# RMSNorm over 16384 rows: squares on ScalarE alone, a third of the rows scaled by GpSimd, and an instruction order written out by hand

## The chip, the cores and the metric

The kernel runs on one core of a Trainium2 chip. The metric is the device time of one execution in microseconds; the median of several executions is given. A core has a VectorE (DVE), a ScalarE (ACT), a GpSimd (POOL), a TensorE (PE) and sixteen DMA engines; SP is the engine that issues most of the transfers here. Each engine works through its own instructions in order, and engines wait for one another by semaphores. SBUF and PSUM are the on-chip memories, both of 128 partitions.

## The reference

```python
x = randn(16, 1024, 512) in float32; gamma = ones(512)

def reference(x, gamma):
    eps = 1e-5
    rms = sqrt(mean(x ** 2, axis=-1, keepdims=True) + eps)
    return x / rms * gamma
```

Each of 16384 rows of 512 numbers is divided by the root of its mean square and multiplied by gamma. The input is read once, 33.5 MB, and the output written once, 33.5 MB.

## The kernel before

The rows are cut into four blocks t = 0 to 3. In a block each of the 128 partitions holds R = 32 neighbouring rows, 64 KB. SBUF has three slots of one block (line 39); blocks 0, 1 and 2 go into slots 0, 1 and 2, and block 3 goes into slot 0 again when block 0 has been stored. The scaling is done in place, so a slot is loaded, scaled and stored.

Work goes in groups of G = 8 rows, 16 groups in all. `row_stats` (line 63) makes the inverse root mean square of a group. It has two ways, in turn. Even groups square row by row on ScalarE, which adds up each row itself (`accum_out`, line 76). Odd groups square four rows at a time into a PSUM tile `sq` (line 70), and VectorE sums each row (line 71). Then ScalarE takes the square root (line 82) and VectorE the reciprocal (line 83). `apply` (line 86) scales the eight rows on VectorE, one `scalar_tensor_tensor` a row (line 88): slot times `rstd`, a number for each partition, times `gamma_b`, gamma spread over all partitions in SBUF. A matmul by a column of ones (line 55) and a copy (line 57) make `gamma_b` at the start.

The last loop computes the statistics of the following group ahead of the scaling of the present one. The framework's scheduler then sets the order on each engine; in the trace, reductions, rows and reciprocals of neighbouring groups are mixed.

`transfers` (line 100) issues all loads and stores on SP's queue, in this order: loads of block 0 (rows 0 to 7, then 8 to 31) at the start; after group (0,0) the store of row 0, the load of block 1, half the load of block 2, the store of row 1, the other half; after block 0's last group its remaining rows in two stores and the load of block 3 in two halves, each of which waits until the store from the same place in slot 0 has landed; after block 1's last group its store (8.4 MB); after block 2's last group its store (8.4 MB); and block 3 in two stores. SP issues in this order, and an issue that must wait holds those behind it.

Of the kernel before, what the change touches and what calls it, by code (L numbers as in the profile page):

```python
# [1 line left out]

# [4 lines left out]


@with_exitstack
def kernel(  # L10
    ctx: ExitStack,
    tc: tile.TileContext,
    x: bass.AP,
    gamma: bass.AP,
    out: bass.AP,
):
    nc = tc.nc
    P = nc.NUM_PARTITIONS
    eps = 1e-5
    fp32 = mybir.dt.float32  # L20
    AF = mybir.ActivationFunctionType
    OP = mybir.AluOpType

    xf = x.flatten_outer_dims()
    of = out.flatten_outer_dims()
    N, D = xf.shape
    R = 32
    G = 8
    H = 4
    assert N == 4 * P * R  # L30

    xv = xf.rearrange("(t p r) d -> t p r d", p=P, r=R)
    ov = of.rearrange("(t p r) d -> t p r d", p=P, r=R)

    const = ctx.enter_context(tc.tile_pool(name="const", bufs=1))
    stats = ctx.enter_context(tc.tile_pool(name="stats", bufs=4))
    psum = ctx.enter_context(tc.tile_pool(name="psum", bufs=2, space=bass.MemoryType.PSUM))

    slots = [const.tile([P, R, D], fp32, name=f"slot{i}") for i in range(3)]

    def load(t, slot, r0, r1):
        nc.sync.dma_start(out=slots[slot][:, r0:r1], in_=xv[t][:, r0:r1])  # L42

    def store(t, slot, r0, r1):
        nc.sync.dma_start(out=ov[t][:, r0:r1], in_=slots[slot][:, r0:r1])

    load(0, 0, 0, 8)
    load(0, 0, 8, 32)

    gamma_row = const.tile([1, D], fp32)  # L50
    nc.scalar.dma_start(out=gamma_row, in_=gamma.unsqueeze(0))
    ones_col = const.tile([1, P], fp32)
    nc.vector.memset(ones_col, 1.0)  # L53
    gamma_psum = psum.tile([P, H, D], fp32, name="sq")
    nc.tensor.matmul(gamma_psum[:, 0], ones_col, gamma_row, start=True, stop=True)  # L55
    gamma_b = const.tile([P, D], fp32)
    nc.vector.tensor_copy(out=gamma_b, in_=gamma_psum[:, 0])  # L57

    eps_t = const.tile([P, 1], fp32)
    nc.vector.memset(eps_t, eps)  # L60
    sq_scratch = const.tile([P, D], fp32)

    def row_stats(slot, g):
        ss = stats.tile([P, G], fp32, name="ss")
        rms = stats.tile([P, G], fp32, name="rms")
        rstd = stats.tile([P, G], fp32, name="rstd")
        if (g // G) % 2:
            for h in range(0, G, H):
                sq = psum.tile([P, H, D], fp32, name="sq")
                nc.scalar.activation(out=sq, in_=slots[slot][:, g + h : g + h + H, :], func=AF.Square)  # L70
                nc.vector.tensor_reduce(  # L71
                    out=ss[:, h : h + H], in_=sq, axis=mybir.AxisListType.X, op=OP.add
                )
        else:
            for r in range(G):
                nc.scalar.activation(  # L76
                    out=sq_scratch,
                    in_=slots[slot][:, g + r, :],
                    func=AF.Square,
                    accum_out=ss[:, r : r + 1],  # L80
                )
        nc.scalar.activation(out=rms, in_=ss, func=AF.Sqrt, bias=eps_t, scale=1.0 / D)  # L82
        nc.vector.reciprocal(out=rstd, in_=rms)  # L83
        return rstd

    def apply(slot, g, rstd):
        for r in range(G):
            nc.vector.scalar_tensor_tensor(  # L88
                out=slots[slot][:, g + r, :],
                in0=slots[slot][:, g + r, :],  # L90
                scalar=rstd[:, r : r + 1],
                in1=gamma_b,
                op0=OP.mult,
                op1=OP.mult,
            )

    groups = [(t, g) for t in range(4) for g in range(0, R, G)]
    slot_of = [0, 1, 2, 0]

    def transfers(t, g):  # L100
        if (t, g) == (0, 0):
            store(0, 0, 0, 1)
            load(1, 1, 0, 32)
            load(2, 2, 0, 16)
            store(0, 0, 1, 2)
            load(2, 2, 16, 32)
        elif (t, g) == (0, 24):
            store(0, 0, 2, 16)
            store(0, 0, 16, 32)
            load(3, 0, 0, 16)  # L110
            load(3, 0, 16, 32)
        elif (t, g) == (1, 24):
            store(1, 1, 0, 32)
        elif (t, g) == (2, 24):
            store(2, 2, 0, 32)
        elif (t, g) == (3, 8):
            store(3, 0, 0, 16)
        elif (t, g) == (3, 24):
            store(3, 0, 16, 32)

    ahead = row_stats(0, 0)
    for k, (t, g) in enumerate(groups):
        rstd = ahead
        if k + 1 < len(groups):
            tn, gn = groups[k + 1]
            ahead = row_stats(slot_of[tn], gn)
        apply(slot_of[t], g, rstd)
        transfers(t, g)


# [1 line left out]
_INS = ['x', 'gamma']  # L132
_OUTS = [((16, 1024, 512), 'float32')]


# [23 lines left out]
```

## Time and profile before

| | |
|---|---|
| median of 3 runs | 162.24 us (162.03 to 162.33) |
| profiled execution, whole | 162.18 us |
| profiled execution, span from first to last instruction | 160.4 us |
| VectorE busy | 122.6 us, 163 instructions |
| ScalarE busy | 80.1 us, 162 instructions |
| GpSimd busy | 0.2 us, 4 instructions |
| TensorE busy | 2.0 us |
| moved by DMA | 67.13 MB, 418 GB/s over the span |
| HBM read and written | 33.56 and 33.55 MB |

The busy time of an engine says how much it worked, not whether the end waited for it. A line of a group gives source line, engine, operation, what it writes and reads with shapes, the count, then the total busy time in us, the mean of one in ns, and the idle time before it with what ended that. A line of the waits gives who waited for whom, the total in us, how often, and the longest. In the slices each digit is the busy share of a fortieth of the span, in tenths. A line of the timeline gives start, duration, engine, line and operation.

### The profile page before, as it was taken

How to read it: one execution, taken by the hardware profiler on the slowest of the kernel's cores; microseconds unless marked ns; L12 is line 12 of the kernel's file. 1: busy time of each engine (PE TensorE's matmuls, PEld its weight loads, DVE VectorE, ACT ScalarE, POOL GpSimd, SP SyncE). 2: the span in 40 equal slices, each digit the busy share in tenths (PEclk: the TensorE clock that was granted, in tenths of full speed). 3: DMA queues.
4: the chain of work that ended last, by engine and by line, in shares of the span. 5: the costliest groups of instructions: out<-in, count | busy, mean ns of one | idle time of the engine just before them, and what ended most of it. 6: DMA issues, size and time to landing. Idle time of an engine off the chain costs nothing.

```text
span 160.4 us, 410 instructions
## 1 busy us (share of the span) xinstructions
PE 2.0 (1%) x2; PEld 0.5 (0%) x2; DVE 122.6 (76%) x163; ACT 80.1 (50%) x162; POOL 0.2 (0%) x4
## 2 busy tenths in 40 slices
PE   4000000000000000000000000000000000000000
PEld 1000000000000000000000000000000000000000
DVE  0100928999999519999999999999999999994000
ACT  3098039990390999996900950079609940000000
POOL 0000000000000000000000000000000000000000
DMA  5999999699699999999999999998998998999993
GB/s 197 523 392 392 466 449 523 261 523 523 262 402 387 455 458 418 453 415 466 409 392 498 409 400 507 409 507 376 425 507 360 441 507 360 417 400 441 449 417 147
DMA packets 2164, 67.13 MB, mean 419 GB/s; under 512 B 241, under 2 KB 241, under 8 KB 498
## 3 DMA queue, kind: packets, MB, share of 16 engines
q1 hardware_dynamic: 2160, 67.11, 97.7%
q14 instruction: 2, 0.02, 0.0%
q10 hardware_dynamic: 2, 0.00, 0.0%
HBM read 33.56 MB, written 33.55 MB: 418 GB/s over the span
## 4 chain that ended last, share of the span: by engine, by line
DVE 67%; DMA 13%; ACT 7%; issue 2%; DVEq 0%; SPq 0%
DVE slot L88 48%; DVE ss L71 18%; DMA slot<-in_x_dram 13%; ACT sq_scratch L76 3%; ACT sq L70 3%; DVE rstd L83 1%; DVEq L154 0%; ACT rms L82 0%; SPq L42 0%
## 5 line engine op out<-in xcount | busy, mean ns | idle before, releaser
L88 DVE SCALAR_TENSOR_TENSOR slot<-slot,rstd,gamma_b 128x512 f32<-128x512 f32 x128 | 85.8, 738 | 0.1
L76 ACT ACTIVATE sq_scratch<-slot 128x512 f32<-128x512 f32 x64 | 40.0, 625 | 10.0 <-DMA slot<-in_x_dram 8.7
L70 ACT ACTIVATE sq<-slot 128x2048 f32<-128x2048 f32 x16 | 29.8, 1864 | 18.6 <-DVE ss L71 11.5
L71 DVE TENSOR_REDUCE ss<-sq 128x4 f32<-128x2048 f32 x16 | 35.9, 2274 | 3.4 <-ACT sq L70 3.4
L82 ACT ACTIVATE rms<-ss,eps_t 128x8 f32<-128x8 f32 x16 | 4.6, 297 | 25.9 <-DVE ss L71 25.7
L83 DVE RECIPROCAL rstd<-rms 128x8 f32<-128x8 f32 x16 | 3.1, 193 | 16.1 <-ACT rms L82 16.1
L76 ACT ACTIVATION_READ_ACCUMULATOR sq_scratch<-slot 128x1 f32 x64 | 11.9, 186 | 0.0
L57 DVE COPY gamma_b<-sq 128x512 f32<-128x512 f32 x1 | 0.7, 691 | 3.3 <-PE sq L55 3.3
L55 PE MATMUL sq<-gamma_row,ones_col 1*128 1x512 f32 x2 | 2.0, 1122 | 2.2 <-DMA gamma_row<-in_gamma_dram 2.2
L76 ACT ACT_TABLE_LOAD x1 | 1.3, 1283 | 1.3 <-PEq L143 1.3
L82 ACT ACT_TABLE_LOAD x1 | 1.3, 1283 | 0.0
L53 DVE MEMSET ones_col<- 1x128 f32 x1 | 0.2, 165 | 0.8 <-PEq L143 0.8
L55 PEld LDWEIGHTS sq<-gamma_row,ones_col 1*128 1x128 f32 x2 | 0.5, 306 | 2.2 <-issue 2.2
L143 POOL MEMSET const-bfloat16-1.0<- 128x1 bf16 x1 | 0.1, 101 | 0.0
L143 POOL MEMSET const-uint8-127<- 128x1 uint8 x1 | 0.1, 101 | 0.0
L143 POOL MEMSET const-float32-0.0<- 128x1 f32 x1 | 0.1, 98 | 0.2 <-issue 0.2
L143 POOL MEMSET const-float32-1.0<- 128x1 f32 x1 | 0.1, 98 | 0.0
L60 DVE MEMSET eps_t<- 128x1 f32 x1 | 0.1, 59 | 0.0
## 6 DMA issues: line engine op xcount, KB each, us to landing
slot<-in_x_dram SPq DMA_DIRECT2D x4, 4096.0 KB, 27.6
out_dram<-slot SPq DMA_DIRECT2D x3, 4096.0 KB, 18.8
slot<-in_x_dram SPq DMA_DIRECT2D x1, 6144.0 KB, 21.5
out_dram<-slot SPq DMA_DIRECT2D x1, 3584.0 KB
slot<-in_x_dram SPq DMA_DIRECT2D x1, 2048.0 KB, 7.2
out_dram<-slot SPq DMA_DIRECT2D x2, 256.0 KB, 21.3
out_dram<-slot SPq DMA_DIRECT2D x2, 29.8
gamma_row<-in_gamma_dram ACTq DMA_DIRECT2D x1, 2.0 KB
```

What stands on the lines that cost most here:

```text
L53: nc.vector.memset(ones_col, 1.0)
L55: nc.tensor.matmul(gamma_psum[:, 0], ones_col, gamma_row, start=True, stop=True)
L57: nc.vector.tensor_copy(out=gamma_b, in_=gamma_psum[:, 0])
L60: nc.vector.memset(eps_t, eps)
L70: nc.scalar.activation(out=sq, in_=slots[slot][:, g + h : g + h + H, :], func=AF.Square)
L71: nc.vector.tensor_reduce(out=ss[:, h : h + H], in_=sq, axis=mybir.AxisListType.X, op=OP.add)
L76: nc.scalar.activation(out=sq_scratch, in_=slots[slot][:, g + r, :], func=AF.Square, accum_out=ss[:, r : r + 1],)
L82: nc.scalar.activation(out=rms, in_=ss, func=AF.Sqrt, bias=eps_t, scale=1.0 / D)
L83: nc.vector.reciprocal(out=rstd, in_=rms)
L88: nc.vector.scalar_tensor_tensor(out=slots[slot][:, g + r, :], in0=slots[slot][:, g + r, :], scalar=rstd[:, r : r + 1], in1=gamma_b, op0=O ...
L143: nc = _bacc.Bacc("TRN2", target_bir_lowering=False, num_devices=1)
```

## The change

Every group's squares are now made on ScalarE without its own sums, 4 to 7 rows an instruction, alternately into one PSUM tile of seven rows (`sq_psum`) and one SBUF tile of five (`sq_sbuf`), and VectorE sums all of them. Groups have 8, 12, 12 and then six times 16 rows; the list gives for each its block, first row, number of rows, the pieces in which it is squared, and the `share`, the number of its last rows that GpSimd scales. GpSimd does this in two instructions a group, by `rstd` and then by gamma. VectorE scales the other rows as before, one by one, but reads gamma from PSUM, where the matmul left it. Shares add up to 48 of 128 rows of a partition.

The scheduler is switched off (`manual_schedule`): on each engine instructions run as written. From the second group on, the squares and reductions of the following group stand ahead of the rows of the present one, and its square root and reciprocal after the third row. VectorE's code begins at an aligned address (`addr_align`). The two memsets of the setup go to GpSimd and the copy of gamma to ScalarE. The transfers keep their sizes and order.

```diff
@@ tile_rmsnorm_eps_1e5_kernel @@
-    G = 8
-    H = 4
...
+    ctx.enter_context(tc.manual_schedule())
+    nc.vector.addr_align(128, offset=0, max_nops=0)
...
-    psum = ctx.enter_context(tc.tile_pool(name="psum", bufs=2, space=bass.MemoryType.PSUM))
+    psum = ctx.enter_context(tc.tile_pool(name="psum", bufs=1, space=bass.MemoryType.PSUM))
...
-    nc.vector.memset(ones_col, 1.0)
-    gamma_psum = psum.tile([P, H, D], fp32, name="sq")
-    nc.tensor.matmul(gamma_psum[:, 0], ones_col, gamma_row, start=True, stop=True)
-    gamma_b = const.tile([P, D], fp32)
-    nc.vector.tensor_copy(out=gamma_b, in_=gamma_psum[:, 0])
+    nc.gpsimd.memset(ones_col, 1.0)
+    gamma_psum = psum.tile([P, D], fp32, name="gamma_psum")
+    nc.tensor.matmul(gamma_psum, ones_col, gamma_row, start=True, stop=True)
+    gamma_b = const.tile([P, 1, D], fp32)
+    nc.scalar.copy(out=gamma_b[:, 0], in_=gamma_psum)
...
-    nc.vector.memset(eps_t, eps)
-    sq_scratch = const.tile([P, D], fp32)
+    nc.gpsimd.memset(eps_t, eps)
-    def row_stats(slot, g):
...
+    groups = [
+        (0, 0, 8, (4, 4), 3),
+        (0, 8, 12, (7, 5), 5),
+        (0, 20, 12, (7, 5), 5),
+        (1, 0, 16, (7, 5, 4), 7),
+        (1, 16, 16, (7, 5, 4), 7),
+        (2, 0, 16, (7, 5, 4), 6),
+        (2, 16, 16, (7, 5, 4), 6),
+        (3, 0, 16, (7, 5, 4), 6),
+        (3, 16, 16, (7, 5, 4), 3),
+    ]
+    slot_of = [0, 1, 2, 0]
+
+    def sum_squares(t, g, n, pieces, share):
+        ss = stats.tile([P, 16], fp32, name="ss")
+        r = 0
+        for k, m in enumerate(pieces):
+            if k % 2:
+                sq = const.tile([P, 5, D], fp32, name="sq_sbuf")
+            else:
+                sq = psum.tile([P, 7, D], fp32, name="sq_psum")
+            rows = slots[slot_of[t]][:, g + r : g + r + m, :]
+            nc.scalar.activation(out=sq[:, :m], in_=rows, func=AF.Square)
+            nc.vector.tensor_reduce(
+                out=ss[:, r : r + m], in_=sq[:, :m], axis=mybir.AxisListType.X, op=OP.add
+            )
+            r += m
+        return ss
+
+    def inverse_rms(ss, n):
+        rms = stats.tile([P, 16], fp32, name="rms")
+        rstd = stats.tile([P, 16, 1], fp32, name="rstd")
+        nc.scalar.activation(out=rms[:, :n], in_=ss[:, :n], func=AF.Sqrt, bias=eps_t, scale=1.0 / D)
+        nc.vector.reciprocal(out=rstd[:, :n, 0], in_=rms[:, :n])
         return rstd
-    def apply(slot, g, rstd):
...
+    def scale_by_pool(rstd, t, g, n, pieces, share):
+        part = slots[slot_of[t]][:, g + n - share : g + n, :]
+        by_row = rstd[:, n - share : n].to_broadcast([P, share, D])
+        nc.gpsimd.tensor_tensor(out=part, in0=part, in1=by_row, op=OP.mult)
+        nc.gpsimd.tensor_tensor(out=part, in0=part, in1=gamma_b.to_broadcast([P, share, D]), op=OP.mult)
+    def scale_row(rstd, t, g, r):
+        x = slots[slot_of[t]][:, g + r, :]
+        nc.vector.scalar_tensor_tensor(
+            out=x, in0=x, scalar=rstd[:, r], in1=gamma_psum, op0=OP.mult, op1=OP.mult
+        )
@@ transfers: the groups' names alone change @@
-        elif (t, g) == (0, 24):
+        elif (t, g) == (0, 20):
...
-    ahead = row_stats(0, 0)
-    for k, (t, g) in enumerate(groups):
-        rstd = ahead
-        if k + 1 < len(groups):
-            tn, gn = groups[k + 1]
-            ahead = row_stats(slot_of[tn], gn)
-        apply(slot_of[t], g, rstd)
+    ready = inverse_rms(sum_squares(*groups[0]), groups[0][2])
+    for k, group in enumerate(groups):
+        t, g, n, pieces, share = group
+        rstd = ready
+        scale_by_pool(rstd, *group)
+        following = groups[k + 1 :][:1]
+        if k > 0:
+            for nxt in following:
+                ss = sum_squares(*nxt)
+        for r in range(n - share):
+            scale_row(rstd, t, g, r)
+            if r == 2 and k > 0:
+                for nxt in following:
+                    ready = inverse_rms(ss, nxt[2])
         transfers(t, g)
+        if k == 0:
+            for nxt in following:
+                ready = inverse_rms(sum_squares(*nxt), nxt[2])
```

After the change, block 0's second part is stored after group (0,20), blocks 1 and 2 after groups (1,16) and (2,16), and block 3 after groups (3,0) and (3,16). In what follows groups are numbered 0 to 8 as in the list.

## The prediction

> **What bounds the kernel now.** I read the slices of the page first, then the DMA queues, then what the DMA queue's own engine (SP) waited for, then the chain of waits, then the costliest groups.
>
> ```profile
> DVE   0100928999999519999999999999999999994000
> ACT   3098039990390999996900950079609940000000
> DMA  5999999699699999999999999998998998999993
> ...
> q1 hardware_dynamic: 2160, 67.11, 97.7%
> ```
>
> All transfers go through one queue, and its packets fill 97.7% of sixteen engines' span. In the packet records the first starts at 1.74 us and the last ends at 159.24 us; in between no engine of the sixteen pauses. The 67.11 MB therefore flow at 67.11/157.5 = 0.426 MB/us, and the queue, served in order, is the bound. VectorE is full from about 60 to 144 us, but only second: it matters where a store that it must release would reach the queue after the queue has run dry. The chain of waits puts 67% on VectorE because it follows the last store back to its producer; that store was still queued behind another one, so this share is no time to be won.
>
> So the view to read is when each store was issued against when the queue needs it. The waits of SP, and its timeline around the store of slot 2:
>
> ```profile
> SPq L45 <- DVE slot L88: 97.9, 7, 29.8
> SPq L42 <- DMA out_dram<-slot: 31.3, 2, 21.9
> 115.83 0.34 SPq L45 DMA_DIRECT2D out_dram<-slot  x1
> ```
>
> SP mostly waits for VectorE rows. The store of t=2 is issued at 115.83. Ahead of it lie all bytes but those of t=2 and t=3 stores: 67.11 - 16.78 = 50.33 MB, gone at 1.74 + 50.33/0.426 = 119.9 us; the records have the sixteen engines taking their first packet of this store between 119.3 and 120.56. The slack is some 4 us, less what an issue takes to become a packet: 1.0 us at the start (issue 0.73, first packet 1.74; all sixteen at work by 2.5). The same sum for the others: store t=1 issued at 85.63, needed at 100.2; first half of t=3 at 131, needed at 139.6; last half at 146.3, needed at 149.4.
>
> Durations and the start of the busy stretch:
>
> ```profile
> L88 DVE SCALAR_TENSOR_TENSOR slot<-slot,rstd,gamma_b 128x512 f32<-128x512 f32 x128 | 85.8, 738 | 0.1
> L71 DVE TENSOR_REDUCE ss<-sq 128x4 f32<-128x2048 f32 x16 | 35.9, 2274 | 3.4 <-ACT sq L70 3.4
> L83 DVE RECIPROCAL rstd<-rms 128x8 f32<-128x8 f32 x16 | 3.1, 193 | 16.1 <-ACT rms L82 16.1
> 22.72 3.68 ACT L70 ACTIVATE sq<-slot 128x2048 f32<-128x2048 f32 x2 [7.13 <-DMA slot<-in_x_dram]
> 24.64 6.69 DVE L71 TENSOR_REDUCE ss<-sq 128x4 f32<-128x2048 f32 x3 [3.38 <-ACT sq L70]
> ```
>
> Instructions overlap by some 0.08 us. From start to start a row costs 0.662 us (15 rows in 9.97), a four-row reduction 2.20 (two in 4.47), a reciprocal 0.11.
>
> [...] In the new kernel the row's second tensor is gamma in PSUM, so I take no contention. [...] the copy of gamma out of PSUM takes 691 ns[...]; the reduction from PSUM 2274[...]; the row from SBUF 738[...].
>
> **The change part by part.**
>
> *DMA.* Bytes, sizes and order on SP's queue stay. Nothing can shorten 157.5 us of packets; the change can only open holes.
>
> *VectorE's work.* All 128 rows are now reduced: 24 reductions of 4, 5 or 7 rows[...]: 3.80 us for seven, 2.73 for five, 2.20 for four. Sum 69.9 against 35.2. Rows scaled on VectorE fall from 128 to 80: 53.0 against 84.7. Reciprocals 1.0 against 1.8. Total 123.9 against 121.7: what GpSimd takes off is given back by reductions. Setup (a copy, two memsets) is off VectorE, under 1 us, under the first load.
>
> *ScalarE.* The 64 squares with accumulator become part of 24 plain ones; seven rows take 1.864 + 1536 x 0.807 ns = 3.10 us (slope from the 625 and 1864 ns rows). It stays under 65 us and hides behind VectorE, but for one place below. The gamma copy lies under the first load, which lands near 7.6.
>
> *GpSimd.* 48 rows twice[...]. It has four groups to do before the store of t=2.
>
> *Group 0.* Two squares and reductions give the reciprocal near 14.7, row 0 near 15.5, some 1 us earlier than now. The queue is full until 22, so this is worth nothing.
>
> *Groups 1 and 2, where the new fixed order costs.* The load of rows 8 to 31 lets ScalarE start at 22.72. Square of 7 rows to 25.82; reductions 7 and 5 from 25.86 to 32.47. ScalarE's Sqrt of group 1 stands in its order ahead of group 2's squares, so those begin at 32.71. On VectorE, group 2's reductions stand ahead of group 1's rows: it idles from the reciprocal, about 33.0, until the square lands at 35.85. Behind the waiting reduction are queued group 1's seven rows, which were ready, and behind them the whole rest. This is the one wait that counts.
>
> *From 35.85 on* VectorE never waits by my sum: each group's square has 1.3 us or more in hand, and the four-row square fits beside the five-row reduction. Group 2's reductions 6.53, group 1's 7 rows 4.63, reciprocal 0.11: 47.1. Then up to the last row of t=2: reductions of five groups at 8.73 = 43.67; rows 7+9+9+10+10 = 45 x 0.662 = 29.79; five reciprocals 0.57. That ends at 121.1, with the pipeline's tail 121.2; SP issues at 121.25 instead of 115.83.
>
> *GpSimd beside it:* reciprocal of group 3 near 58.0, then 26 rows back to back[...].
>
> *At the queue.* First packets 1.0 to 1.8 us after the issue: 122.3 to 123.1. Each engine still has 8 x 2.42 + 16 x 1.21 = 38.7 us to move, so they end at 161.0 to 161.8 instead of 159.24: 1.8 to 2.5 us late; I take 2.0. Other stores: t=0 at 47.2 and 60.7 (needed at 62 and 71), t=1 at 90.3 (100.2), t=3 at 136.7 and 145.3 (some 141.6 and 151.4 after the delay). All in time, so the hole is paid once.
>
> *Costs with two ends.* A row with gamma in PSUM: between 48 ns less (693 is the shortest row in the trace, 741 the median)[...]; 52 such rows lie before the issue[...]; I take 0, as the PSUM rows above show no surcharge. Reductions from the SBUF scratch: 0 to 0.04 us more (a reciprocal's fixed cost is 0.1), seven of them, 0.3. Instruction fetch for the new alignment: 0 to one packet's wait, 2.4; no stall shows on VectorE now, so 0. [...]
>
> Sum: span 160.4 + 2.0 = 162.4, plus 1.78 around it (162.18 - 160.40) = 164.2. The profiled run stands 0.06 below the median of 162.24, which is nothing here. Forecast 164.2 us, 1.2% slower.
>
> **Rivals.**
>
> *A, dearer VectorE or a fetch stall.* [...] a stall of 2.4 us falls in the full stretch: [...] every microsecond goes into the hole[...]. [...] Against: the 691 ns copy.
>
> *B, GpSimd is the bound.* [...]
>
> *C, no change.* The store of t=2 comes in time. One mechanism: the row's fixed cost falls with one operand out of SBUF. Place: the 52 rows before the issue. Price: up to 48 ns each, 2.5 us. It decides from about 1.9/52 = 36 ns on, when SP issues by 119.4; then nothing is left of the hole, and the time is 162.2. For it: the shortest rows. Against: the median.
>
> *D, faster.* Only faster packets or an earlier first one could do it; 0.3 us would be needed, and no part of the change touches either.
>
> **Chances.** Forecast 0.55, A 0.18, B 0.09, C 0.14, D 0.04. The measurement tells about 0.2% (0.3 us) from no change. Slower 0.82, same 0.14, faster 0.04. The likeliest case alone spans 163.2 to 165.4; the range that also takes in C and most of A is 162.1 to 167.2.
>
> **What would show it.** After: VectorE idle for about 3 us ahead of the reduction near 36, released by a square; SP's store of t=2 at 121.2; a slice of low DMA share there, and q1's share down to about 96.6%; rows still near 738 ns[...]. The steps fall if rows are under 700 ns, if the store's issue is released by GpSimd, or if the DMA has its hole elsewhere. A q1 share still near 97.7% would make the forecast wrong.

## The result, and the profile after

The changed kernel takes 165.00 us (median of 4 runs, 164.86 to 165.15) against 162.17 us before: a ratio of 1.0174 (95% interval 1.0156 to 1.0192), 2.8 us or 1.7% slower. Its profiled execution takes 164.93 us, with a span of 163.3 us.

The page of the changed kernel, the slices of two engines and of the DMA, and the queue's share:

```profile
DVE  0037803939999999999999999999999999970000
POOL 1000770059979749999999993999199749100000
DMA  5999989979989998999999899996909959889885
...
q1 hardware_dynamic: 2160, 67.11, 96.2%
q14 instruction: 1, 0.01, 0.0%
```

The DMA slices have a 0 where before they had a 9: the thirtieth slice, 118.4 to 122.5 us. The queue's share of the span is down from 97.7% to 96.2% though the bytes are the same. Stretches of 2 us around that place (the length, then busy us and instructions of PE, PEld, DVE, ACT and POOL, then clock, DMA share, GB/s) show a hole, a time in which the queue is empty:

```profile
116.00:118.00 2.00, 0.00 (x0) 0.00 (x0) 2.00 (x5) 2.00 (x1) 0.40 (x1) 1.00 1.21 524
118.00:120.00 2.00, 0.00 (x0) 0.00 (x0) 2.00 (x5) 2.00 (x2) 2.00 (x1) 1.00 0.08 33
120.00:122.00 2.00, 0.00 (x0) 0.00 (x0) 2.00 (x5) 1.04 (x1) 2.00 (x1) 1.00 0.00 0
122.00:124.00 2.00, 0.00 (x0) 0.00 (x0) 2.00 (x2) 0.00 (x0) 1.92 (x2) 1.00 1.23 524
```

(A packet is put down where it starts, so a stretch can read over 1.) VectorE is full throughout; the transfers wait for it. In SP's timeline the store of block 2 is issued here:

```profile
122.12 0.34 SPq L46 DMA_DIRECT2D out_dram<-slot  x1
```

That is 6.3 us later than before (115.83). VectorE's timeline shows where the lateness begins:

```profile
27.11 3.89 DVE L87 TENSOR_REDUCE ss<-sq_psum 128x7 f32<-128x3584 f32 x1 [6.56 <-ACT sq_psum L86]
30.91 2.81 DVE L87 TENSOR_REDUCE ss<-sq_sbuf 128x5 f32<-128x2560 f32 x1
34.09 0.23 DVE L97 RECIPROCAL rstd<-rms 128x12 f32<-128x12 f32 x1 [0.37 <-ACT rms L96]
37.14 3.89 DVE L87 TENSOR_REDUCE ss<-sq_psum 128x7 f32<-128x3584 f32 x1 [2.82 <-ACT sq_psum L86]
```

The last line is group 2's reduction, which stands ahead of group 1's rows and waits 2.82 us for a square. From there to the end of block 2 VectorE has no gap. Two of the costliest groups of the changed kernel:

```profile
L103 POOL TENSOR_TENSOR slot<-slot,rstd 128x3072 f32<-128x3072 f32 (+3 forms) x9 | 42.7, 4740 | 41.4 <-DVE rstd L97 41.4
...
L108 DVE SCALAR_TENSOR_TENSOR slot<-slot,rstd,gamma_psum 128x512 f32<-128x512 f32 x80 | 53.2, 727 | 0.0
```

GpSimd idles 41.4 us for VectorE's reciprocals, so it isn't the bound. A row costs 727 ns, as good as the 738 before.

One thing isn't explained by this: the loads land late. ScalarE's first squares in the changed kernel:

```profile
8.82 1.88 ACT L86 ACTIVATE sq_psum<-slot 128x2048 f32<-128x2048 f32 x1 [4.00 <-DMA slot<-in_x_dram]
...
23.91 3.16 ACT L86 ACTIVATE sq_psum<-slot 128x3584 f32<-128x3584 f32 x1 [7.02 <-DMA slot<-in_x_dram]
```

Before, they began at 7.98 and 22.72 (the line of the latter stands in the prediction):

```profile
7.98 0.63 ACT L76 ACTIVATE sq_scratch<-slot 128x512 f32<-128x512 f32 x1 [5.43 <-DMA slot<-in_x_dram]
```

The trace also records when each of the sixteen DMA engines reports its part of a transfer. The table gives, for some transfers, how far the last engine is behind the median one, in us:

| transfer (median landing) | before | after |
|---|---|---|
| rows 0-7 of block 0 (7.8) | 0.23 | 0.95 |
| rows 8-31 of block 0 (22.6) | 0.16 | 1.33 |
| block 2, second half (63.0) | 0.53 | 2.82 |
| block 3, second half (100.6) | 0.92 | 2.83 |
| store of block 1 (120.0) | 0.90 | 2.77 |
| last store (158.7, after 162.2) | 0.91 | 0.09 |

In the changed kernel one engine falls behind in the first load and is 2.8 us late by 63 us (in these loads the last but one is within 0.3 us of the median); only the hole at 120 us, in which it catches up, makes it even with the others. So there are two suspects, the hole and the late engine. The records also show one fetch of 8 KB of instructions by DMA at 3.8 us; before, there were two, at 46.9 and 64.7.

The packet records give no engine's number, but they show what this fetch does. It takes 0.31 us and starts as one 16 KB packet of the load ends; when it ends, another 16 KB packet starts, and that one takes 1.14 us where 0.61 is usual. By these times one engine served the fetch between its own packets, and lost 0.31 + 0.53 = 0.84 us by it, about the lateness of the first load. All sixteen such fetches within the spans of the twelve kernels here stand like this between two packets, and the packet after the fetch is 0.28 to 0.65 us longer than others of its size.

### The profile page after: what moved, and what is told of

It reads as the page before. It is cut to its first block, busy times and chain, and to the rows that moved or that the text cites. A ratio compares the mean times of both kernels' runs of the same rounds, so it can differ in the third digit from the quotient of the medians.

```text
span 163.3 us, 275 instructions
## 1 busy us (share of the span) xinstructions
PE 2.0 (1%) x2; PEld 0.5 (0%) x2; DVE 123.8 (76%) x113; ACT 63.5 (39%) x36; POOL 96.6 (59%) x24
## 3 DMA queue, kind: packets, MB, share of 16 engines
q1 hardware_dynamic: 2160, 67.11, 96.2%
## 4 chain that ended last, share of the span: by engine, by line
DVE 67%; DMA 14%; ACT 4%; issue 4%; DVEq 0%; SPq 0%
DVE ss L87 38%; DVE slot L108 29%; DMA slot<-in_x_dram 14%; ACT sq_psum L86 4%; DVE rstd L97 1%; DVEq L176 0%; SPq L43 0%; ACT rms L96 0%
## 5 line engine op out<-in xcount | busy, mean ns | idle before, releaser
L103 POOL TENSOR_TENSOR slot<-slot,rstd 128x3072 f32<-128x3072 f32 (+3 forms) x9 | 42.7, 4740 | 41.4 <-DVE rstd L97 41.4
L87 DVE TENSOR_REDUCE ss<-sq_psum 128x7 f32<-128x3584 f32 (+1 forms) x15 | 47.0, 3131 | 20.1 <-ACT sq_psum L86 20.1
L104 POOL TENSOR_TENSOR slot<-slot,gamma_b 128x3072 f32<-128x3072 f32 (+3 forms) x9 | 53.6, 5951 | 0.7
L108 DVE SCALAR_TENSOR_TENSOR slot<-slot,rstd,gamma_psum 128x512 f32<-128x512 f32 x80 | 53.2, 727 | 0.0
L86 ACT ACTIVATE sq_psum<-slot 128x3584 f32<-128x3584 f32 (+1 forms) x15 | 38.3, 2555 | 34.9 <-DVE ss L87 23.8
L87 DVE TENSOR_REDUCE ss<-sq_sbuf 128x5 f32<-128x2560 f32 (+1 forms) x9 | 24.7, 2744 | 0.0
L86 ACT ACTIVATE sq_sbuf<-slot 128x2560 f32<-128x2560 f32 (+1 forms) x9 | 20.5, 2274 | 0.0
L96 ACT ACTIVATE rms<-ss,eps_t 128x16 f32<-128x16 f32 (+2 forms) x9 | 2.8, 306 | 27.1 <-DVE ss L87 27.0
L97 DVE RECIPROCAL rstd<-rms 128x16 f32<-128x16 f32 (+2 forms) x9 | 2.1, 230 | 2.1 <-ACT rms L96 2.1
L56 PE MATMUL gamma_psum<-gamma_row,ones_col 1*128 1x512 f32 x2 | 2.0, 1122 | 2.2 <-DMA gamma_row<-in_gamma_dram 2.2
```

The lines of the kernel that those rows point to most:

```text
L56: nc.tensor.matmul(gamma_psum, ones_col, gamma_row, start=True, stop=True)
L86: nc.scalar.activation(out=sq[:, :m], in_=rows, func=AF.Square)
L87: nc.vector.tensor_reduce(out=ss[:, r : r + m], in_=sq[:, :m], axis=mybir.AxisListType.X, op=OP.add)
L96: nc.scalar.activation(out=rms[:, :n], in_=ss[:, :n], func=AF.Sqrt, bias=eps_t, scale=1.0 / D)
L97: nc.vector.reciprocal(out=rstd[:, :n, 0], in_=rms[:, :n])
L103: nc.gpsimd.tensor_tensor(out=part, in0=part, in1=by_row, op=OP.mult)
```

## The experiments

All times are medians; ratios are to the kernel before in the same comparison (162.07 to 162.14 us).

### The store of block 2 in two halves

```diff
+        elif (t, g) == (2, 0):
+            store(2, 2, 0, 16)
         elif (t, g) == (2, 16):
-            store(2, 2, 0, 32)
+            store(2, 2, 16, 32)
```

> The changed kernel with the store of block 2 cut in two: the first half is issued after group 5, the second after group 6. VectorE, GpSimd and ScalarE work as before. Theory 1, the hole in the queue near 120 us is the whole loss: it goes, and the time is that of the kernel before, 162.2. Theory 2, hole and a late DMA engine: in the changed kernel one of the sixteen engines runs 2.8 us behind the others from 63 us on, and the hole only hid it; without the hole the late engine sets the end, 158.67 + 2.8 + some 0.1 for the last landing against 162.32 now, so 0.9 less than 165.0: 164.1. Theory 3, GpSimd's traffic slows the transfers as a whole: 165.0 stays.

163.99 us (1.0110, 1.0061 to 1.0160). The issues are at 106.5 and 121.9, VectorE is as late as ever, and the hole is gone. The late engine is 2.55 us behind at 120 us and still 2.54 at 149: nothing lets it catch up, and it sets the end. Theory 2 holds: of the 2.8 us lost, closing the hole alone returns 1.0.

### VectorE's code not aligned

```diff
-    nc.vector.addr_align(128, offset=0, max_nops=0)
```

> The changed kernel without the line that aligns VectorE's code. Theory: the fetch of 8 KB of instructions at 3.8 us comes from it, delays one DMA engine in the first load by 0.8 us, and so the landing of the first loads by 1.0 to 1.2 us. Without it ScalarE starts at 8.0 and 22.7 instead of 8.8 and 23.9, the store of block 2 is issued near 120.9, and the time falls to 163.8. Rival: the late engine has another cause; the landings stay late and the time is 165.0, or later by up to 2 us if VectorE then stalls for instructions in its full stretch.

163.93 us (1.0103, 1.0056 to 1.0150). ScalarE's timeline in this run:

```profile
7.91 1.88 ACT L85 ACTIVATE sq_psum<-slot 128x2048 f32<-128x2048 f32 x1 [3.00 <-DMA slot<-in_x_dram]
...
22.89 3.16 ACT L85 ACTIVATE sq_psum<-slot 128x3584 f32<-128x3584 f32 x1 [6.91 <-DMA slot<-in_x_dram]
```

The loads are on time again, the last engine is 0.2 us behind until 81 us, and everything on VectorE is 1.0 us earlier; the store of block 2 is issued at 121.09. The fetch is now at 89.2 us, and from there one engine is late by 0.9, then 1.4 us.

### One line in the kernel before

Aligned code and nothing else, added to the kernel before:

```diff
+    nc.vector.addr_align(128, offset=0, max_nops=0)
     const = ctx.enter_context(tc.tile_pool(name="const", bufs=1))
```

> The kernel before with the one line that aligns VectorE's code, and nothing else. If the fetch of instructions[...] makes one DMA engine late, it is seen at about 3.8 us, the first loads land some 1 us later, one engine stays 1 to 2.8 us behind to the end, and the time is 163.0 to 164.0 though VectorE's rows and reductions are as before. If the lateness needs the new order or GpSimd's work: 162.1.

164.76 us (1.0147, 1.0099 to 1.0195): a line that computes nothing costs 2.6 us, more than expected. VectorE's order and durations are those of before; its group of rows:

```profile
L89 DVE SCALAR_TENSOR_TENSOR slot<-slot,rstd,gamma_b 128x512 f32<-128x512 f32 x128 | 85.8, 739 | 0.1
```

ScalarE's timeline has the first load landing 1.0 us late:

```profile
8.97 0.63 ACT L77 ACTIVATE sq_scratch<-slot 128x512 f32<-128x512 f32 x1 [6.41 <-DMA slot<-in_x_dram]
```

Fetches are at 4.0, 48.2 and 101.8 us. One engine is 1.24 us behind in the first load, 2.6 at 63 us, 3.6 at 100 us, and 3.24 at the end. The rise at 100 us is the last fetch: it lies between two packets of the late engine, which lands the transfer only at 104.3. There is no hole at 120 us (the store of block 2 is issued at 117.6, in time); ahead of the last store, issued at 148.0, the engines that are on time pause for up to 0.6 us. So the late engine costs without the new order and without GpSimd.

### Where the fetch falls

Two kernels give `addr_align` another offset than 0, to see whether the fetch moves (the offsets are called slots here; they have nothing to do with the slots of SBUF). That the fetch would come near 46 and 71 us was the author's estimate. To keep the hole out, both have GpSimd take four rows more ahead of the store of block 2, which was first tried without alignment:

```diff
-        (0, 8, 12, (7, 5), 5),
-        (0, 20, 12, (7, 5), 5),
+        (0, 8, 12, (7, 5), 6),
+        (0, 20, 12, (7, 5), 6),
...
-        (2, 0, 16, (7, 5, 4), 6),
-        (2, 16, 16, (7, 5, 4), 6),
+        (2, 0, 16, (7, 5, 4), 7),
+        (2, 16, 16, (7, 5, 4), 7),
```

> The changed kernel without the alignment, and GpSimd takes one row more in each of the groups 1, 2, 5 and 6; transfers as in the changed kernel. If VectorE's amount of work ahead of the store of block 2 makes the hole, four rows less bring its issue from 121.1 to 118.5, ahead of the dry queue, GpSimd being done by 114.5: 162.6, as with the store cut in two. If the store waits for something else: 163.9.

162.56 us (1.0024, 1.0011 to 1.0037); the store is issued at 118.38, and no hole is left. Then with the code aligned to slot 108, and to slot 86:

```diff
+    nc.vector.addr_align(128, offset=108, max_nops=0)
```

> The kernel with GpSimd's four rows more (share 6, 6 and 7, 7 in groups 1, 2 and 5, 6), with VectorE's code aligned to slot 108 of a block of 128 instead of slot 0[...]. No hole is expected, so the end tells the lateness of the DMA engine that serves the fetch. If it is the fetch that makes an engine late, the first loads land on time (7.9 and 22.8), the lateness begins near 46 us, and with the 0.9 us at the end that the kernel before has with fetches at 47 and 65 us the time is 162.1. If any alignment makes the first load late: 163.5 or more.

> The same with slot 86[...], near 71 us. The lateness begins there; at the end 0.9 to 1.4 us, as after the fetch at 88 us without alignment: 162.1 to 162.6.

Slot 108: 163.70 us (1.0084, 1.0053 to 1.0115), the fetch at 42.3 us. The first loads land on time (ScalarE at 7.98 and 22.94), and the lateness begins at the fetch, as expected; but it grows to 2.2 us at the end, not 0.9, so the time was missed by 1.6 us. Slot 86: 162.22 us (1.0001, 0.9987 to 1.0015), the fetch at 73.5 us, 1.25 us late at the end.

The store cut in two and no alignment were also put together:

> The changed kernel with both single edits: the store of block 2 in two halves, and no alignment of VectorE's code. Theory, the loss is the hole plus one late DMA engine: the hole is gone, and what is left of the lateness is the 1.4 us that one engine had after the fetch at 89.2 us, so the last landing comes at 158.5 + 1.4 = 159.9 instead of 161.3, and the time is 162.6. If only the hole mattered: 162.1. If the two edits were the same gain twice: 163.9.

162.80 us (1.0041, 1.0029 to 1.0053). With it there are seven kernels without the hole at 120 us, that of before among them. The lateness in the table is the last engine's against the median one, in the profiled execution, at the last store (at the store that lands near 149 us where block 2's store is cut in two). In two kernels the engines that are on time pause late in the kernel, on average for 0.2 to 0.3 us, while the late one goes on; for these the lateness ahead of the pause is added:

| kernel | first fetch, us | last engine late, us | time, us |
|---|---|---|---|
| before | 46.9 | 0.9 | 162.1 |
| GpSimd four rows more, slot 86 | 73.5 | 1.25 | 162.22 |
| GpSimd four rows more, no alignment | 87.9 | 1.4 | 162.56 |
| store in two halves, no alignment | 89.3 | 1.6 | 162.80 |
| GpSimd four rows more, slot 108 | 42.3 | 2.2 (2.5 ahead of the pause) | 163.70 |
| store in two halves, slot 0 | 3.6 | 2.5 | 163.99 |
| before, slot 0 | 4.0 | 3.2 (3.6 ahead of the pause) | 164.76 |

Time follows lateness one for one to within 0.3 us. Against the kernel before, the last line is 2.7 us later and 2.7 us slower, slot 108 is 1.6 and 1.6.

### Four rows less on GpSimd

```diff
-        (2, 0, 16, (7, 5, 4), 6),
-        (2, 16, 16, (7, 5, 4), 6),
+        (2, 0, 16, (7, 5, 4), 4),
+        (2, 16, 16, (7, 5, 4), 4),
```

> The changed kernel with the shares of groups 5 and 6 lowered from 6 to 4: four rows more on VectorE, 4 x 0.66 = 2.64 us, ahead of the store of block 2. If the hole grows with the lateness one for one: issue at 124.7 and 165.0 + 2.6 = 167.6. If GpSimd's load is what costs, its 8 rows less make it faster or leave 165.0.

168.53 us (1.0382, 1.0336 to 1.0428), 3.5 more than the changed kernel. SP's timeline has the issue where it was expected:

```profile
124.57 0.34 SPq L46 DMA_DIRECT2D out_dram<-slot  x1
```

The hole grew by 2.45 us with it (the median engine's last landing by 2.47). The other 0.9 us was not foreseen: a second fetch came at 140.3 us, after the hole, and one engine was 0.9 us late at the end. The changed kernel has no second fetch within its span; what brought this one isn't shown.

### Rows of group 1 ahead of the reductions

```diff
-        if k > 0:
+        if k > 1:
             for nxt in following:
                 ss = sum_squares(*nxt)
         for r in range(n - share):
             scale_row(rstd, t, g, r)
-            if r == 2 and k > 0:
+            if r == 3 and k == 1:
+                for nxt in following:
+                    ss = sum_squares(*nxt)
+            if r == (6 if k == 1 else 2) and k > 0:
```

> The changed kernel with four rows of group 1 ahead of group 2's reductions on VectorE, and the reciprocal of group 2 after the last row. If the wait of 2.8 us near 34 to 37 is what makes the store of block 2 late, the store is issued near 119.4 instead of 122.1 and the hole shrinks to under 1 us for most engines; the time is 162.8 if the hole is everything, 164.1 if the late DMA engine then sets the end. If VectorE's wait cost nothing (the time given back elsewhere), the store is still issued near 122 and the time stays at 165.0.

164.08 us (1.0108, 1.0060 to 1.0155), but not for the expected reason. VectorE's timeline:

```profile
34.71 2.72 DVE L108 SCALAR_TENSOR_TENSOR slot<-slot,rstd,gamma_psum 128x512 f32<-128x512 f32 x4
37.49 3.89 DVE L87 TENSOR_REDUCE ss<-sq_psum 128x7 f32<-128x3584 f32 x1
...
47.53 3.89 DVE L87 TENSOR_REDUCE ss<-sq_psum 128x7 f32<-128x3584 f32 x1 [1.31 <-ACT sq_psum L86]
```

The wait near 35 is filled with four rows, but the next group's square is then not ready and VectorE waits 1.31 us at 47.5. That square stands behind the root of group 2, at 44.14, which needs the reduction just done; block 1 landed at 44.25 in this run, so the transfer would have let it start no earlier. Of 2.8 us only 0.8 came through: issue at 121.30, time 0.9 less.

### Gamma from SBUF for VectorE's rows

```diff
-            out=x, in0=x, scalar=rstd[:, r], in1=gamma_psum, op0=OP.mult, op1=OP.mult
+            out=x, in0=x, scalar=rstd[:, r], in1=gamma_b[:, 0], op0=OP.mult, op1=OP.mult
```

> The changed kernel with VectorE's rows reading gamma from SBUF instead of PSUM, so that a row has two SBUF tensors while GpSimd reads SBUF. If the two exclude each other[...], a row that starts beside a GpSimd instruction waits for its end, up to 7.8 us, or GpSimd waits; from group 3 on rows and GpSimd no longer overlap, and the time is 175 to 190. If there is no contention, rows take 738 ns instead of 727, the store of block 2 is 0.3 to 0.6 us later, and the time is 165.0 to 165.6.

237.81 us (1.4658, 1.4576 to 1.4739), far above the expected range. The group of rows, GpSimd's first multiplications, then a piece of the timeline:

```profile
L108 DVE SCALAR_TENSOR_TENSOR slot<-slot,rstd,gamma_b 128x512 f32<-128x512 f32 x80 | 136.2, 1765 | 0.0
L103 POOL TENSOR_TENSOR slot<-slot,rstd 128x3072 f32<-128x3072 f32 (+3 forms) x9 | 45.2, 5019 | 107.8 <-DVE rstd L97 107.8
```

```profile
95.63 6.52 POOL L103 TENSOR_TENSOR slot<-slot,rstd 128x3584 f32<-128x3584 f32 x1 [12.16 <-DVE rstd L97]
96.05 16.77 DVE L108 SCALAR_TENSOR_TENSOR slot<-slot,rstd,gamma_b 128x512 f32<-128x512 f32 x5
102.23 8.05 POOL L104 TENSOR_TENSOR slot<-slot,gamma_b 128x3584 f32<-128x3584 f32 x1
```

Five rows take 16.77 us. Taken singly, the first starts at 96.05, takes 6.64 us and ends 0.55 us after GpSimd's first instruction; the second starts at 102.62, takes 8.21 us and ends 0.55 us after GpSimd's second; the other three take 0.74 each. So a row stands through one GpSimd instruction, and one row gets in between the two. With the row's second operand in PSUM there is none of this: 727 ns beside a busy GpSimd. The estimate was low because only rows and GpSimd were taken to exclude each other. In VectorE's fixed order the reductions stand behind the blocked rows, and the next reciprocal behind them, and GpSimd now idles 107.8 us for reciprocals, against 41.4.

## Why the prediction was right, and where its size was off

*The queue is the bound, nothing to win.* It held. Without the hole, and with an engine late by 1.25 us only, the new arrangement is level with the kernel before (162.22, ratio 1.0001), and no kernel was faster.

*VectorE's work, 123.9 us.* Measured 123.8; reductions of seven, five and four rows took 3.80, 2.73 and 2.20 us from start to start, as put down. *Rows at 0.662 us, PSUM no dearer:* 0.658 from start to start (median), and a four-row reduction took 2276 ns from PSUM and from SBUF alike, so rivals A and C had no ground. *GpSimd off the path (rival B):* held; its two passes over seven rows took 6.16 and 7.76 us, and its last instruction ahead of the store of block 2 ended at 114.28, 7.8 us ahead of VectorE's last row (122.04). *No contention with gamma in PSUM:* held, at 727 ns a row with GpSimd at work (749 at most), where rows with gamma in SBUF took 738 beside an idle one. With gamma in SBUF and GpSimd at work a row took 1765 ns on average, and the kernel 237.81 us, 73 more than the changed kernel. *Group 0:* its reciprocal was put near 14.7 and came at 16.93, as the load landed 1 us late and ScalarE's table load ahead of the square root (1.28 us, at 15.30) was left out; with the queue full until 22 this cost nothing.

*The one wait that counts, from about 33.0 to 35.85.* It is there, 2.82 us, ending at 37.14. From it to the end of block 2 the sum gave 85.3 us; it took 84.8.

*The hole, paid once.* It is there and nowhere else. First packets were expected 1.0 to 1.8 us after the issue; they came 0.84 after it, all sixteen within 0.15 us (122.96 to 123.11). From the first of them to the last packet 39.0 us pass, in this kernel, in the one without alignment and in the one with rows first alike (38.7 expected).

*The term that was mis-sized.* The prediction said of the DMA that bytes, sizes and order stay and that the change can only open holes, and it let ScalarE start at 22.72 as before. For the alignment it looked at a stall of VectorE and took 0. No stall came, but the fetch that alignment moved to 3.8 us went between the packets of one DMA engine and made it late in the first load. ScalarE started at 23.91, 1.2 us late, while VectorE was 0.4 faster than the sum: issue 122.12 instead of 121.25, and the last packet 2.7 us later than before instead of 2.0. That is the 0.8 us between 164.2 and 165.0; that VectorE's gain hid some of the lateness is luck. Undoing the alignment returned 1.07 us and all of the late landing, so this is shown and not only argued.

*The hole is only part of the loss.* Closed alone, it left 164.0, since the late engine then set the end. Undone alone, hole and alignment return 1.0 and 1.1 us; together 2.2 of the 2.8 (162.80).

What stays open: why an engine once late falls further behind at certain places (in the changed kernel from 1.3 to 1.9 us at 52 us and to 2.8 at 63, and by some 0.5 near 99 us without alignment). Each time it is one long packet: in the changed kernel 1.82 us at 50.8 and 2.55 at 61.7, where 1.21 is usual for its size. Packets of other engines lengthen near 61 us too, but less (1.58 to 1.73 us). In the kernel without alignment engines that are on time pass the first two places unharmed. Nor is it recorded whose instructions a fetch brings: that they are VectorE's rests on the fetch moving with the alignment of VectorE's code (slot 0: 3.6 to 4.0 us; 108: 42.3; 86: 73.5; none, in the new order: 87.9 to 89.3). A kernel of this length without any fetch was not made.

## What to carry to other kernels

Where transfers are the bound, write down for each one when the queue needs it and when its producer releases it; an edit costs nothing until one of these turns negative, and from there it costs one for one (here an issue at 118.38 us left no hole, and one 2.45 us later than 122.12 made the hole 2.45 us longer). Here cutting the transfer in two closed the hole by an edit of three lines, while rows put into the producer's wait moved the store by 0.8 of 2.8 us. In an order written by hand, look for an instruction that waits ahead of ones that are ready, and count what is queued behind it. And compare the slowest DMA engine with the median one: in the full queue here it set the end (2.5 us behind with the store in two halves), and one line that aligns code made it late (by 0.95 us in the first load of the changed kernel, by 1.24 in the kernel before).

## What the runs showed of the hardware

- A fetch of 8 KB of instructions took 0.31 us between two packets (by their times, of one DMA engine), and the packet after it took 0.28 to 0.65 us more than usual (sixteen fetches in twelve kernels). With `addr_align(128, offset=0, max_nops=0)` on VectorE one came at 3.6 to 4.0 us, in all six kernels with that line.
- An engine that was late in a full queue didn't catch up: 2.55 us behind at 120 us, 2.54 at 149, with the store in two halves. In the changed kernel the hole put all sixteen level: 2.77 us before it, 0.09 to 0.11 after it.
- With both tensors in SBUF a row stood through one GpSimd instruction at a time (6.64 us beside one of 6.52, 8.21 beside one of 8.05); with one tensor in PSUM it took 727 ns beside them.
- GpSimd's multiplication by a number per row took 1.72 ns an element (6.16 us for 3584), by a full vector 2.17 (7.76 us).
